# A fused decoder layer on one core: two sets of transposes go from TensorE to VectorE and small DMAs, and a state load is requested later

## The chip, the core and the metric

The kernel runs on one core of a Trainium2 chip. The metric is the device time of one execution in microseconds (us), as the median of three runs. The text calls the engines TensorE (PE, with its weight loads as PEld), VectorE (DVE), ScalarE (ACT), GpSimd (POOL) and SyncE (SP, which issues nearly all DMAs).

## What is computed

One layer of a decoder, in float32, for 256 prompt tokens with 16 meta tokens ahead of them and for 8 new tokens that each continue a stored state. The model width is 2048.

```
x <- LN1(alpha*x + 0.5*SwiGLU_1(x))
x <- LN2(alpha*x + Mixer(x))
x <- LN3(alpha*x + 0.5*SwiGLU_2(x))

Mixer: x @ w_in -> q_ret k_ret v_ret g_ret | q_hg f_hg i_hg g_hg | gate_ret gate_hg
  retention (8 heads of 256): S <- gamma*S + k^T v, o = (q k^T * decay) v + q S
  HGRN2 (16 heads of 128):    f = lb + (1-lb)*sigmoid(f_hg), k = 1 - f, q = silu(q_hg), v = i_hg
                              S <- f*S + k^T v, o = q S
  y = sigmoid(gate_ret)*LN(o_ret)*silu(g_ret) + sigmoid(gate_hg)*RMS(o_hg)*silu(g_hg);  y @ w_out
```

The outputs are the layer's result and both kinds of states, for the prompt and for the 8 new tokens.

## The kernel before, in words

**Dense products.** Activations lie with features on the partitions and the 280 tokens (16 + 256 + 8; 264 where the meta tokens are not needed) along the free axis. Every weight block of 128 x 128 and every activation tile is split into a high and a low part (`whi`, `wlo`; `xh`, `xl`), and `dense` issues three matmuls for a block: high x high, high x low, low x high (L218). Weights stream in loads of 8 blocks, 512 KB each, through three buffers: SP issues the DMA into `raw` (L185), ACT writes `whi` (L188), DVE writes `wlo` = `raw` - `whi` (L189), and PE then has 24 matmuls of such a load. A new `raw` can be issued when `wlo` of the load three before it is written.

**The mixing, by units.** `project` runs eight units u = 0 to 7, one retention head and two HGRN2 heads each. A unit is six groups of two 128-wide columns in the order f, q_h, i_h, q_r, k_r, v_r, and behind them come the four gate groups of the unit before: g_r/a_r, g_h/a_h, g_r/a_r, g_h/a_h. A group is 16 k-steps of six matmuls, four weight loads; a unit with its gates is 40 loads. `evacuate` takes a finished group out of PSUM.

**What sets the order.** The heads' own work is written as two generators, `mix_hg` (HGRN2) and `mix_ret` (retention), which `start` puts on a list with a delay. After each k-step `dense` calls `pump`, which counts every generator down by one and lets it issue its next piece at zero; a `yield n` is a pause of n k-steps. PE keeps exactly the order in which its instructions are written. The other engines' orders, SP's too, are set by a scheduler from priorities and from when it expects the operands; each engine then runs in order, and an instruction that waits holds up all behind it. A DMA completes on one of eight semaphores in turn, and an issue waits until the DMA that used its semaphore before has landed.

**HGRN2, unit u, before.** The evacuation of i_h copies the two heads' values to `v` (L667, L668) and starts `mix_hg` four k-steps later. It needs the values and the scaled keys `K` with tokens on the partitions. PE transposes the values, two blocks of 128 x 128 for each head (L875), into PSUM, and ACT copies them to `vt` (L879). The first and last 16 tokens of the values (`ends`, gathered by POOL) are transposed as one more block (L878). For K, `turned` does the same on PE (L982) and ACT (L983) into `kts`. These transposes are single matmuls against an identity. Then the state products `pst` = K^T v run on PE (L1022, L1024), ACT and DVE make the states `Sh` of them (L1025, L1027), and SP stores them (`out_sgp`). `samples` updates the 8 stored states of each head; `load` and `values` request what it needs, each held back by a one-column POOL copy into the buffer to be filled, which reads a tile that marks the time.

**Retention, unit u, before.** `mix_ret` starts three k-steps after v_r was evacuated. It requests the first half of the unit's stored states, two loads of 512 KB (`smr`, L1095), without a mark, so the scheduler puts them in SP's order as soon as the four `smr` buffers come free, behind the stores of the unit before (`out_srs`, L1202). Then come its transposes (L1107, L1114), scores (`psc`), state products (`psr`, L1168), and the update of the stored states: ACT scales them (L1192), DVE adds to them (L1198).

Of the kernel before, what the change touches and what calls it, by code (L numbers as in the profile page):

```python
# [18 lines left out]
P = 128  # L19
# [4 lines left out]
NMETA, SEQ, NS = 16, 256, 8  # L24
LP = NMETA + SEQ
T = LP + NS
# [102 lines left out]
def trunk(ctx: ExitStack, tc: tile.TileContext, A, O):  # L129
# [417 lines left out]
    with tc.tile_pool(name="yp", bufs=1) as yp:  # L547
# [7 lines left out]
        with tc.tile_pool(name="mp", bufs=1) as mp:  # L555
# [92 lines left out]
            def evacuate(n, c0, c1, o0, o1, b0, b1):  # L648
# [14 lines left out]
                elif n == "i_h":  # L663
                    v = st.pop("i_h", None)
                    if v is None:
                        v = tmp("v", (P, 2, T))
                        nc.scalar.copy(v[:, 0, :], o0)  # L667
                        nc.scalar.copy(v[:, 1, :], o1)  # L668

                    start(mix_hg(c0 // 2, st["f"], st["k"], st["q"], v), {0: 20, 2: 46}.get(c0, 4))  # L670
                elif n in ("q_r", "k_r"):
# [10 lines left out]
                elif n == "v_r":  # L682
                    v = tmp("v", (P, 2, T))
                    nc.scalar.copy(v[:, 0, :], o0)
                    nc.scalar.copy(v[:, 1, :], o1)
                    start(mix_ret(c0 // 2, st["q_r"], st["k_r"], v), 24 if c0 == 2 else 3)
                elif n in ("g_r", "g_h"):
# [14 lines left out]
                    else:  # L702
# [6 lines left out]
                        if c0 < EARLY:  # L709
                            split(yh[c0], yl[c0], y)  # L710

            NB2 = LP - 2 * P
            BLOCKS = ((0, P), (P, P), (2 * P, T - 2 * P))
# [31 lines left out]

            def mix_hg(u, f, k, q, v):

                calm = 2
                ends = tmp("ends", (P, 2, 2, NMETA))
                nc.gpsimd.tensor_copy(ends[:, :, 0, :], v[:, :, :NMETA])  # L750
                nc.gpsimd.tensor_copy(ends[:, :, 1, :], v[:, :, T - NMETA :])
                Q = tmp("Q", (P, 2, SEQ))
# [12 lines left out]
                def load(h):  # L765

                    sms.append(tmp("smh", (P, NS, P), bufs=2))
                    vbs.append(tmp("vbh", (P, NS, P), bufs=2))
                    nc.gpsimd.tensor_copy(sms[h][:, 0, :1], kts[0][:, 0, :1] if h else acc[:, 15:16])
                    nc.sync.dma_start(sms[h], A["sg"][2 * u + h])  # L770

                def values(h):
                    nc.gpsimd.tensor_copy(vbs[h][:, 0, :1], kts[1][:, 0, :1] if h else acc[:, 2 * P + 15 : 2 * P + 16])
                    nc.sync.dma_start(vbs[h], vrow[h].partition_broadcast(P))
# [93 lines left out]
                Q1 = side_by_side(1)  # L868
                vt = tmp("vth", (P, 2, 2, P))
                vrow = []  # L870
                for h in range(2):

                    pt = mx_bank("pt")
                    for b in range(2):
                        nc.tensor.transpose(pt[:, b * P : (b + 1) * P], v[:, h, NMETA + b * P : NMETA + (b + 1) * P], ident)  # L875
                    x = pt[:64, 2 * P : 3 * P]
                    if h:
                        nc.tensor.transpose(x, ends.rearrange("p c a t -> p (c a t)"), ident)  # L878
                    nc.scalar.copy(vt[:, h], pt[:, : 2 * P].rearrange("p (b f) -> p b f", b=2))  # L879
# [93 lines left out]
                on_h[u] = on  # L973
                kts = []

                def turned(h):
                    kt = tmp("kth", (P, 2, P), bufs=2)
                    kts.append(kt)
                    pt = mx_bank("ptk")
                    for b in range(2):  # L980
                        t0 = NMETA + b * P
                        nc.tensor.transpose(pt[:, b * P : (b + 1) * P], K[:, h, t0 : t0 + P], ident)  # L982
                    nc.scalar.copy(kt, pt[:, : 2 * P].rearrange("p (b f) -> p b f", b=2))  # L983
# [29 lines left out]
                if u != 1:  # L1013
                    samples(1)
                    yield 4 if u == 0 else 5

# [68 lines left out]
            def mix_ret(u, q, k, v):  # L1085
# [103 lines left out]
                for e in range(2):  # L1189
# [187 lines left out]
```

## Time and profile before

| what | value |
|---|---|
| runs, device time | 2566.4, 2569.12, 2565.67 us; median 2566.4 |
| profiled execution, first to last instruction | 2563.9 us |
| between that span and the median of the runs | 2.5 us |
| mean granted TensorE clock | 1.000 |
| PE, DVE, ACT, POOL busy, share of the span | 100%, 66%, 54%, 2% |
| DMA queue of SP | 532.37 MB, 62.0% of 16 engines' span |

The profile is of one execution. A row of the groups reads: line, engine, operation, out<-in, shape, count | busy us, mean ns of one | idle time of the engine before them, and what ended it. A row of the waits reads: engine and line <- what it waited for: us in total, times, longest. A row in order of time reads: start, length, engine, line, operation, out<-in, shape, count, all in us from the span's start. Matmul records overlap, since PE starts the next before the last has left the array: their lengths do not add up to time, their starts do. Line numbers are those of the kernel before.

### The profile page before, as it was taken

What the parts mean: (1) busy time and instruction counts of PE and PEld (TensorE: products, weight loads), DVE (VectorE), ACT (ScalarE), POOL (GpSimd) and SP (SyncE); (2) the same over time, 40 slices, a digit from 0 to 9 for tenths busy, and PEclk for the clock granted to TensorE, in tenths of its full rate; (3) what the DMA queues carried; (4) which work ended last, traced back from release to release, by engine and by line L of the source; (5) the groups of instructions that cost most, each with busy time, mean ns of one, the idle gap of its engine ahead of it and who ended that gap; (6) DMA issues with size and microseconds to landing.
All of it is one profiled execution on the core that took longest, in us unless ns stands there. A gap on an engine that the chain in (4) does not pass through costs nothing.

```text
span 2563.9 us, 56275 instructions
## 1 busy us (share of the span) xinstructions
PE 2553.4 (100%) x23424; PEld 2534.4 (99%) x23424; DVE 1702.8 (66%) x2827; ACT 1392.2 (54%) x2186; POOL 57.0 (2%) x152
## 2 busy tenths in 40 slices
PE   9999999999999999999999999999999999999999
PEld 9999999999999999999999999999999999999998
DVE  6444544475569878777777777777885555556555
ACT  5444444444456767767676666675564444444443
POOL 0000000000000000000000000000000000000000
PEclk9999999999999999999999999999999999999999
DMA  7555555555555876767676767675556565565554
GB/s 244 183 187 183 187 182 184 186 182 186 184 201 180 287 265 232 264 214 260 212 264 215 259 223 255 224 239 188 196 190 197 194 197 195 194 196 195 195 195 149
DMA packets 156897, 536.26 MB, mean 209 GB/s; under 512 B 17952, under 2 KB 25952, under 8 KB 156640
## 3 DMA queue, kind: packets, MB, share of 16 engines
q1 hardware_dynamic: 156352, 532.37, 62.0%
q8 instruction: 183, 3.00, 0.5%
q14 instruction: 74, 0.61, 0.1%
q10 hardware_dynamic: 288, 0.29, 0.0%
HBM read 501.99 MB, written 30.61 MB: 208 GB/s over the span
## 4 chain that ended last, share of the span: by engine, by line
PE 96%; DVE 2%; ACT 0%; issue 0%; DMA 0%; SPq 0%; ACTq 0%; DVEq 0%
PE up L218 36%; PE dn L218 19%; PE pj_i_h L218 3%; PE pj_g_r L218 3%; PE pj_q_h L218 3%; PE pj_g_h L218 3%; PE pj_a_r L218 3%; PE pj_a_h L218 3%; PE pj_f L218 3%; PE pj_q_r L218 3%; PE pj_k_r L218 3%; PE wo L218 3%; PE pj_v_r L218 3%; DVE wlo L189 1%; PE pqr L1211 1%; PE psr L1168 0%
## 5 line engine op out<-in xcount | busy, mean ns | idle before, releaser
L189 DVE TENSOR_TENSOR wlo<-raw,whi 128x1024 fp32r<-128x1024 f32 (+1 forms) x869 | 1062.2, 1223 | 740.7 <-ACT whi L188 737.3
L188 ACT CAST whi<-raw 128x1024 fp32r<-128x1024 f32 (+1 forms) x870 | 905.7, 1042 | 909.2 <-PE up L218 411.0
L218 PE MATMUL up<-xh,whi 128*128 128x280 f32 (+1 forms) x2624 | 725.6, 280 | 0.6 <-ACT whi L188 0.6
L218 PE MATMUL up<-xh,wlo 128*128 128x280 f32 (+1 forms) x2624 | 725.8, 280 | 0.4 <-DVE wlo L189 0.3
L218 PE MATMUL up<-xl,whi 128*128 128x280 f32 (+1 forms) x2624 | 725.4, 279 | 0.0
L218 PEld LDWEIGHTS up<-xh,wlo 128*128 128x128 f32 x2624 | 492.6, 189 | 1.0 <-DVE wlo L189 1.0
L218 PEld LDWEIGHTS up<-xh,whi 128*128 128x128 f32 x2624 | 492.6, 189 | 0.8 <-ACT whi L188 0.8
L218 PEld LDWEIGHTS up<-xl,whi 128*128 128x128 f32 x2624 | 492.6, 189 | 0.0
L218 PE MATMUL dn<-hh,whi 128*128 128x280 f32 (+1 forms) x1376 | 384.7, 280 | 0.0
L218 PE MATMUL dn<-hh,wlo 128*128 128x280 f32 (+1 forms) x1376 | 384.3, 279 | 0.0
L218 PE MATMUL dn<-hl,whi 128*128 128x280 f32 (+1 forms) x1376 | 384.3, 279 | 0.0
L218 PEld LDWEIGHTS dn<-hh,whi 128*128 128x128 f32 x1376 | 260.1, 189 | 0.1
L218 PEld LDWEIGHTS dn<-hl,whi 128*128 128x128 f32 x1376 | 260.1, 189 | 0.1
L218 PEld LDWEIGHTS dn<-hh,wlo 128*128 128x128 f32 x1376 | 260.1, 189 | 0.0
L218 PE MATMUL pj_k_r<-xh,whi 128*128 128x280 f32 x256 | 74.2, 290 | 0.0
L218 PE MATMUL pj_g_r<-xh,whi 128*128 128x264 f32 x256 | 74.0, 289 | 0.0
L218 PE MATMUL pj_v_r<-xh,whi 128*128 128x280 f32 x256 | 73.8, 288 | 0.0
L218 PE MATMUL pj_v_r<-xh,wlo 128*128 128x280 f32 x256 | 72.4, 283 | 0.3 <-DVE wlo L189 0.3
L218 PE MATMUL pj_g_h<-xh,whi 128*128 128x264 f32 x256 | 72.7, 284 | 0.0
L218 PE MATMUL pj_k_r<-xh,wlo 128*128 128x280 f32 x256 | 72.4, 283 | 0.0
L218 PE MATMUL pj_v_r<-xl,whi 128*128 128x280 f32 x256 | 72.3, 283 | 0.0
L218 PE MATMUL pj_k_r<-xl,whi 128*128 128x280 f32 x256 | 72.3, 283 | 0.0
(421 smaller groups left out, 5263.4 us busy)
## 6 DMA issues: line engine op xcount, KB each, us to landing
raw<-in_w_up SPq DMA_DIRECT2D x343, 512.0 KB, 4.1
raw<-in_w_in SPq DMA_DIRECT2D x320, 512.0 KB, 4.3
raw<-in_w_dn SPq DMA_DIRECT2D x172, 512.0 KB, 3.5
smr<-in_sr SPq DMA_DIRECT2D x32, 512.0 KB, 5.0
out_srs<-smr SPq DMA_DIRECT2D x32, 512.0 KB, 6.7
raw<-in_w_out SPq DMA_DIRECT2D x32, 512.0 KB, 3.9
vbr<-vrd SPq DMA_DIRECT2D x32, 256.0 KB, 4.1
smh<-in_sg SPq DMA_DIRECT2D x16, 512.0 KB, 5.2
```

The costliest lines, as they stand in the source:

```text
L188: nc.scalar.copy(hi[:, j:jn, :], raw[:, j:jn, :])
L189: nc.vector.tensor_tensor(out=lo[:, j0:j1, :], in0=raw[:, j0:j1, :], in1=hi[:, j0:j1, :].bitcast(F32), op=ALU.subtract)
L218: nc.tensor.matmul(o, w, t, start=start, stop=stop)
L1211: nc.tensor.matmul(pq[32 * j : 32 * j + 32, :256], qdr_at[c][:, 32 * b : 32 * b + 32], sms[2 * e + c][:, j, :], start=e + c == 0, stop=e + ...
```

## The change

From unit 2 on (the third unit):

- The evacuation of i_h no longer copies `v`. DVE transposes the two heads' 256 prompt tokens out of PSUM, in blocks of 32 x 32, into the tile `v`, and ACT copies the first and last 16 tokens of each head to `ends` (four copies of 16 columns).
- A 32 x 32 block is then turned but not at its place in the 128 x 128 block. `turned_over` puts it there by 16 DMAs on SP, each of 32 partitions x 4 runs of 32 elements (16 KB in runs of 128 bytes), one every two k-steps.
- K is turned in the same way by one DVE transpose of 512 columns at the place of the first PE transpose, into the tile that held `k`; 16 DMAs bring it into the tile that held `f`, which is `kts` now.
- PE's transposes of values and K go, with ACT's copies behind them. The one of `ends` stays.
- The pauses: `pst` comes 30 k-steps behind `samples(1)` instead of 5, and 20 instead of 45 follow it.
- Retention starts 5 k-steps after v_r instead of 3, and its pause before the sample scores is 13 instead of 15. Its first two state loads are marked by a POOL copy that reads `q`, so they go out only when the q_h group of their unit, which is the unit that follows the stores, has been evacuated.
- The POOL marks of HGRN2's second head read the turned `k` and a piece of `f`.

```diff
 elif n == "i_h":
-    v = st.pop("i_h", None)
-    if v is None:
+    v, vt = st.pop("i_h", None), tmp("vth", TURNED)
+    ends = tmp("ends", (P, 2, 2, NMETA))
+    if c0 > 2:
+        z = squared(tmp("v", (P, 2, T)))
+        for j, o in enumerate((o0, o1)):
+            nc.vector.transpose(z[:, j].rearrange("p b t -> p (b t)"), o[:, NMETA:LP])
+            nc.scalar.copy(ends[:, j, 0, :], o[:, :NMETA])
+            nc.scalar.copy(ends[:, j, 1, :], o[:, T - NMETA : T])
+        turned_over(vt, z, 2)
+    elif v is None:
...
-    start(mix_ret(c0 // 2, st["q_r"], st["k_r"], v), 24 if c0 == 2 else 3)
+    start(mix_ret(c0 // 2, st["q_r"], st["k_r"], v), {0: 3, 2: 24}.get(c0, 5))
...
+def turned_over(out, z, pause):
+
+    def transfers():
+        for i in range(0, P, 32):
+            for j in range(0, P, 32):
+                nc.sync.dma_start(out[j : j + 32, :, :, i : i + 32], z[i : i + 32, :, :, j : j + 32])
+                yield pause
+
+    start(transfers(), 1)
...
-    nc.gpsimd.tensor_copy(sms[h][:, 0, :1], kts[0][:, 0, :1] if h else acc[:, 15:16])
+    nc.gpsimd.tensor_copy(sms[h][:, 0, :1], (kts[0] if u < 2 else k)[:, 0, :1] if h else acc[:, 15:16])
...
-    kts = []
+    kts = [squared(f)[:, h] for h in range(2)] if u > 1 else []

     def turned(h):
+        if u > 1:
+            if h == 0:
+                z = squared(k)
+                nc.vector.transpose(z.rearrange("p h b t -> p h (b t)"), K[:, :, NMETA:])
+                turned_over(squared(f), z, 2)
+            return
...
     if u != 1:
         samples(1)
-        yield 4 if u == 0 else 5
+        yield 4 if u == 0 else 30
...
-    yield (8, 11, 45)[min(u, 2)]
+    yield (8, 11, 20)[min(u, 2)]
...
 def load(e):
     for c in range(2):
         sms.append(tmp("smr", (P, 4, 256), bufs=4))
+        if e == 0 and u > 1:
+            nc.gpsimd.tensor_copy(sms[c][:, 0, :1], st["q"][:, 0, :1])
         nc.sync.dma_start(sms[2 * e + c], A["sr"][u, c, :, 4 * e : 4 * e + 4, :])
...
-    yield (11 if u == 0 else 15) + 2 * calm
+    yield (11, 15, 13)[min(u, 2)] + 2 * calm
```

PE before, unit 4, at k-step 9 of the k_r group (`pj_k_r` are the group's two columns, `ptk` the transpose of K):

```order
L218 MATMUL pj_k_r_16261<-xh_9_9271,wlo_16376 128x280
L218 MATMUL pj_k_r_16262<-xh_9_9271,whi_16375 128x280
L218 MATMUL pj_k_r_16262<-xl_9_9272,whi_16375 128x280
L218 MATMUL pj_k_r_16262<-xh_9_9271,wlo_16376 128x280
L982 MATMUL ptk<-ident,K 128x128 x2
L218 MATMUL pj_k_r_16261<-xh_10_9275,whi_16375 128x280
```

After, the same place without it, in unit 4:

```order
L218 MATMUL pj_k_r_16304<-xh_9_9271,wlo_16423 128x280
L218 MATMUL pj_k_r_16305<-xh_9_9271,whi_16422 128x280
L218 MATMUL pj_k_r_16305<-xl_9_9272,whi_16422 128x280
L218 MATMUL pj_k_r_16305<-xh_9_9271,wlo_16423 128x280
L218 MATMUL pj_k_r_16304<-xh_10_9275,whi_16422 128x280
```

The pair is gone and nothing is in its stead; the same holds at step 13 and, for the values, at steps 3 and 4 of the q_r group.

PE before, unit 4, at k-step 13 of the v_r group, and after, behind k-step 6 of the first g_h/a_h gate group (`pst` are the state products; they read `f` for the turned keys now):

```order
L218 MATMUL pj_v_r_16461<-xh_13_9287,wlo_16598 128x280
L1022 MATMUL pst<-vm,km 128x128
L1024 MATMUL pst<-vth,kth 128x128 x2
L1022 MATMUL pst<-vm,km 128x128
L1024 MATMUL pst<-vth,kth 128x128 x2
L218 MATMUL pj_v_r_16460<-xh_14_9291,whi_16597 128x280
```

```order
L218 MATMUL pj_a_h_16896<-xh_6_9259,wlo_16974 128x264
L1050 MATMUL pst<-vm,km 128x128
L1052 MATMUL pst<-vth,f 128x128 x2
L1050 MATMUL pst<-vm,km 128x128
L1052 MATMUL pst<-vth,f 128x128 x2
L218 MATMUL pj_g_h_16895<-xh_7_9263,whi_16973 128x264
```

The ten matmuls of this row group (a float32 product is two matmuls, a float32r one is one) stand 25 k-steps later.

SP before and after, unit 4, over the same weight loads, which are the 31st to the 34th counted from the unit's first (`f<-k` are pieces of K, `vrd`, `vbr`, `out_srp` and `smr` retention's):

```order
L185 DMA raw_16972<-in_w_in 128x1024
L1156 DMA vbr<-vrd 128x512 x2
L185 DMA raw_17002<-in_w_in 128x1024
L1171 DMA out_srp<-sro 128x256
L185 DMA raw_17044<-in_w_in 128x1024
L1095 DMA smr<-in_sr 128x1024
L1171 DMA out_srp<-sro 128x256
L1095 DMA smr<-in_sr 128x1024
L185 DMA raw_17074<-in_w_in 128x1024
```

```order
L185 DMA raw_17020<-in_w_in 128x1024
L741 DMA f<-k 32x4x32 x5
L185 DMA raw_17062<-in_w_in 128x1024
L741 DMA f<-k 32x4x32
L749 DMA vrd<-vt_8636 8x256
L185 DMA raw_17104<-in_w_in 128x1024
L1186 DMA vbr<-vrd 128x512 x2
L1201 DMA out_srp<-sro 128x256
L1125 DMA smr<-in_sr 128x1024
L185 DMA raw_17134<-in_w_in 128x1024
```

The last six K pieces are ahead of the second and third of these weight loads, and retention's transfers are one to two loads later than before.

More of the change, by code (lines that the diff above doesn't have):

```diff
@@ L668, in evacuate @@
                         nc.scalar.copy(v[:, 1, :], o1)
-                    start(mix_hg(c0 // 2, st["f"], st["k"], st["q"], v), {0: 20, 2: 46}.get(c0, 4))
+                    start(mix_hg(c0 // 2, st["f"], st["k"], st["q"], v, ends, vt), {0: 20, 2: 46}.get(c0, 4))
                 elif n in ("q_r", "k_r"):
@@ L744, in sample_columns, with mix_hg @@
                     po[:, 3 * P :].rearrange("p (j c) -> p c j", c=32)[:, : 2 * n, :].rearrange("p (h e) j -> p h e j", e=2))
[L746 removed]
+            def mix_hg(u, f, k, q, v, ends, vt):
                 calm = 2
[L749 to L751 removed]
+                if u < 2:
+                    nc.gpsimd.tensor_copy(ends[:, :, 0, :], v[:, :, :NMETA])
+                    nc.gpsimd.tensor_copy(ends[:, :, 1, :], v[:, :, T - NMETA :])
                 Q = tmp("Q", (P, 2, SEQ))
@@ L768, in load @@
                     vbs.append(tmp("vbh", (P, NS, P), bufs=2))
-                    nc.gpsimd.tensor_copy(sms[h][:, 0, :1], kts[0][:, 0, :1] if h else acc[:, 15:16])
+                    nc.gpsimd.tensor_copy(sms[h][:, 0, :1], (kts[0] if u < 2 else k)[:, 0, :1] if h else acc[:, 15:16])
                     nc.sync.dma_start(sms[h], A["sg"][2 * u + h])
                 def values(h):
-                    nc.gpsimd.tensor_copy(vbs[h][:, 0, :1], kts[1][:, 0, :1] if h else acc[:, 2 * P + 15 : 2 * P + 16])
+                    n = 32 if h and u > 1 else P
+                    nc.gpsimd.tensor_copy(vbs[h][:n, 0, :1], kts[1][:n, 0, :1] if h else acc[:, 2 * P + 15 : 2 * P + 16])
                     nc.sync.dma_start(vbs[h], vrow[h].partition_broadcast(P))
@@ L868, in mix_hg @@
                 Q1 = side_by_side(1)
-                vt = tmp("vth", (P, 2, 2, P))
                 vrow = []
                 for h in range(2):
[L873 to L876, printed above, removed]
+                    if u < 2 or h:
+                        pt = mx_bank("pt")
+                    if u < 2:
+                        for b in range(2):
+                            nc.tensor.transpose(pt[:, b * P : (b + 1) * P], v[:, h, NMETA + b * P : NMETA + (b + 1) * P], ident)
                     if h:
+                        x = pt[:64, 2 * P : 3 * P]
                         nc.tensor.transpose(x, ends.rearrange("p c a t -> p (c a t)"), ident)
-                    nc.scalar.copy(vt[:, h], pt[:, : 2 * P].rearrange("p (b f) -> p b f", b=2))
+                    if u < 2:
+                        nc.scalar.copy(vt[:, h], pt[:, : 2 * P].rearrange("p (b f) -> p b f", b=2))
                     if h:
```

2 lines of the change are left out of this document (added).

## The prediction

> **What bounds the kernel now.** I read the page's busy times and chain first, then what TensorE (PE) waited for, then one unit's stretch, then single instructions.
>
> ```profile
> span 2563.9 us, 56275 instructions
> PE 2553.4 (100%) x23424; PEld 2534.4 (99%) x23424; DVE 1702.8 (66%) x2827; ACT 1392.2 (54%) x2186; POOL 57.0 (2%) x152
> ...
> PE 96%; DVE 2%; ACT 0%; issue 0%; DMA 0%; SPq 0%; ACTq 0%; DVEq 0%
> ```
>
> PE is busy for the whole span and is 96% of the chain that ended last. A busy PE need not be at its peak, so the next view is the list of what PE waited for, over the whole span:
>
> ```profile
> PE pw L515 <- DVE eps_h L163: 1.0, 1, 1.0
> PE pt L1116 <- POOL tails L1103: 0.9, 1, 0.9
> ...
> PE pj_v_r L218 <- DVE wlo L189: 0.3, 1, 0.3
> ```
>
> These are the two longest and a typical one of nine rows, together under 5 us in 2563.9. Asked for 980 to 1738 us alone, units 2 to 7, the same list is empty: there PE waits for nothing. One of those units (unit 4 in its mixing, 126 us) in the table by stage:
>
> ```profile
> 1232.00:1358.00 126.00, 126.00 (x1273) 124.33 (x1272) 98.18 (x193) 84.37 (x157) 6.18 (x14) 1.00 0.71 239
> ```
>
> The columns after the length are PE, PEld, DVE, ACT, POOL, the granted clock, the DMA share and GB/s. PE 126.00 of 126.00, clock 1.00, DVE 98.18. So an instruction taken out of PE's order there shortens the span by the time it holds the order up, as long as nothing else becomes late.
>
> **The change, part by part.** *Transposes leave PE.* In units 2 to 7 go four transposes of values (L875) and four of K (L982) each: 48, in 24 pairs. The groups by line, all eight units:
>
> ```profile
> L875 PE MATMUL pt<-ident,v 128*128 128x128 f32 x32 | 6.1, 273 | 0.0
> L982 PE MATMUL ptk<-ident,K 128*128 128x128 f32 x32 | 6.1, 273 | 0.0
> ```
>
> 273 ns is one record's length, but records overlap: what counts is how much later the next matmul starts. PE in order of time around one pair:
>
> ```profile
> 1266.08 0.28 PE L218 MATMUL pj_k_r<-xh,wlo 128*128 128x280 f32 x1
> ...
> 1266.43 0.28 PE L218 MATMUL pj_k_r<-xh,wlo 128*128 128x280 f32 x1
> 1266.56 0.38 PE L982 MATMUL ptk<-ident,K 128*128 128x128 f32 x2
> 1266.69 0.37 PE L218 MATMUL pj_k_r<-xh,whi 128*128 128x280 f32 x1
> 1266.89 0.28 PE L218 MATMUL pj_k_r<-xl,whi 128*128 128x280 f32 x1
> ...
> 1267.49 0.28 PE L218 MATMUL pj_k_r<-xh,whi 128*128 128x280 f32 x1
> ...
> 1268.68 0.28 PE L218 MATMUL pj_k_r<-xl,whi 128*128 128x280 f32 x1
> ```
>
> From 1266.08 to 1267.49, ten projection matmuls and the pair: 1.41. From 1267.49 to 1268.68, ten without: 1.19. The pair costs 0.22 us; both differences are rounded to 0.01, so 0.21 to 0.24. I take 0.225: 24 x 0.225 = **5.4 us**, bounds 24 x 0.21 = 5.0 and 24 x 0.24 = 5.8. The transpose of `ends` (64 rows) stays and is in neither.
>
> The Trainium skill says otherwise of the price: "TensorE: Matmul & The Clock Gate", Part 4 (PE-mode transpose), gives about 275 ns for a transpose in a kernel's context, which agrees with the 273 ns of a record here; summed by it the 48 would be worth an estimated 13.2 us. The spacing of the starts, not the record, decides between the two.
>
> *Copies and transposes on ACT and VectorE (DVE).* The rows for what goes and for the nearest of what comes:
>
> ```profile
> L668 ACT COPY v<-pj_i_h 128x280 f32<-128x280 f32 x7 | 2.8, 393 | 0.0
> L879 ACT COPY vth<-pt 128x256 f32<-128x256 f32 x16 | 5.6, 367 | 0.0
> L983 ACT COPY kth<-ptk 128x256 f32<-128x256 f32 x16 | 6.0, 373 | 8.2 <-PE ptk L982 8.1
> L1120 ACT COPY vt<-pt 24x128 f32<-24x128 f32 x16 | 4.1, 259 | 0.3
> L1083 DVE TENSOR_TENSOR vtr<-vtr,cen 128x512 f32<-128x512 f32 x8 | 5.5, 692 | 0.3
> L1083 DVE TENSOR_TENSOR osr<-osr,cen 128x256 f32<-128x256 f32 x8 | 3.4, 425 | 0.3
> ```
>
> Per unit ACT loses 2 x 0.393 (the row is one evacuation of two), 2 x 0.367 and 2 x 0.373, 2.3 us, and gains four small `ends` copies, at most 4 x 0.259 = 1.0: 1.3 us less. DVE gains two transposes of 256 columns and one of 512: no row shows one, and the nearest of the same sizes give 2 x 0.425 + 0.692 = 1.5 us; twice that would be 3.1. Either end fits in DVE's 126.00 - 98.18 = 28 us of room, and they stand ahead of the unit's tightest stretch (below), not in it. I price both at 0 on the path; without that room it would be up to 1.5 to 3.1 us a unit.
>
> *Thirty-two DMAs of 16 KB a unit on SP.* They finish what a 32 x 32 transpose leaves undone. Two questions: are weights (`raw`) late behind them, and are the turned pieces there when PE wants them. An issue, and what lands when:
>
> ```profile
> 1293.85 0.33 SPq L185 DMA_DIRECT2D raw<-in_w_in  x1
> ...
> 1302.99 0.33 SPq L185 DMA_DIRECT2D raw<-in_w_in  x1
> ```
> ```profile
> raw<-in_w_in SPq DMA_DIRECT2D x320, 512.0 KB, 4.3
> ...
> out_sgp<-Sh SPq DMA_DIRECT2D x16, 64.0 KB, 4.8
> ```
>
> At 0.33 us an issue, 32 are 10.6 us of SP's 126 a unit, at most six (2.0 us) between two weight loads, which come about one per 2.7 us or slower. In the order each issue also waits until the DMA eight issues before it has landed, 4.3 us for a `raw`. Against that stands the lead: the load that is read from 1312.2 on (below, counted at 24 projection matmuls to a load) was issued at 1302.99, 9 us ahead, and that is among the latest of the unit. Cost 0, up to 0.5 us a unit if not.
>
> For the second question: in SP's new order the last K piece stands behind the `raw` that before was issued at 1293.85, so it is out by about 1294.2 and, landing like the 64 KB store of 512-byte runs, there by 1299.0. PE wants it behind step 6 of the first g_h/a_h group, which ends where step 7 begins:
>
> ```profile
> 1303.39 0.28 PE L218 MATMUL pj_g_h<-xh,whi 128*128 128x264 f32 x1
> ```
>
> 4.4 us to spare: cost 0. The values' pieces are all issued ahead of the K pieces, whose start is the old place of L982 (1266.56); the buffer they are read from is next written after the v_r group, still running at 1282.64 (below). Cost 0. Behind PE's wait for a late piece stands its whole order; behind SP's, all weight loads.
>
> *The state matmuls and retention move.* The ten `pst` matmuls go from v_r step 13 into the gates, with two ACT copies and four DVE updates behind them; retention starts two steps later and gives them back at its last pause. Moved, they cost PE the same. What they push is the weight split in the gates, which is the tightest place of the unit:
>
> ```profile
> 1298.66 0.28 PE L218 MATMUL pj_g_h<-xh,whi 128*128 128x264 f32 x1
> ...
> 1312.39 0.28 PE L218 MATMUL pj_g_r<-xh,wlo 128*128 128x264 f32 x1
> ```
> ```profile
> 1310.97 1.22 DVE L189 TENSOR_TENSOR wlo<-raw,whi 128x1024 fp32r<-128x1024 f32 x1
> ```
> ```profile
> 1281.29 0.28 PE L218 MATMUL pj_v_r<-xh,wlo 128*128 128x280 f32 x1
> ...
> 1282.64 0.28 PE L218 MATMUL pj_v_r<-xl,whi 128*128 128x280 f32 x1
> ```
> ```profile
> L1027 DVE SCALAR_TENSOR_TENSOR Sh<-Sh,T,pst 128x128 f32<-128x128 f32 x32 | 9.1, 342 | 0.2
> L1025 ACT COPY Sh<-pst 128x128 f32<-128x128 f32 x16 | 3.5, 266 | 0.2
> ```
>
> Five loads of 24 matmuls (2.70 us each) after 1298.66, the sixth load's `wlo` is finished at 1312.19 and first read at 1312.39: 0.2 us to spare. Into this stretch go 4 x 0.342 = 1.4 us of DVE and 0.5 of ACT; PE gets there later by the ten `pst`, 1282.64 - 1281.29 less two matmuls of 0.12 = 1.1. So DVE loses 1.4 - 1.1 = 0.3 against 0.2 to spare. For it speaks that retention's own order changes: the weight casts now stand ahead of the two state scalings that ACT used to do first. I take 0; the other end is 1 us a unit.
>
> *First state loads behind the queries.* Two loads of 512 KB a unit move from right behind the last state stores to the q_h/i_h groups; nothing is added. POOL marks them, SP then issues; behind POOL's wait stand the marks for the HGRN2 states, much later. Loads cost PE nothing where they were, though ACT did wait for weights:
>
> ```profile
> ACT whi L188 <- DMA raw<-in_w_in: 40.7, 27, 3.1
> ```
>
> 40.7 us of such waits and none passed on to PE in units 2 to 7: 0, either sign, up to 0.5 us a unit (with the 32 DMAs above).
>
> **Sum.** 2563.9 - 5.4 = 2558.5 for the span. The median of the runs, 2566.4, is 2.5 above the profiled span, and nothing outside the span changes: 2566.4 - 5.4 = **2561.0 us**. 0.2% of this kernel, about what a measurement can tell from no change, is 5.1 us; the forecast is just past it.
>
> **The rivals.** *The gates' weight split becomes late* (0.2 us to spare, 0.3 lost): PE waits 0.5 to 1 us a unit, 3 to 6 in all: 2564 to 2567. Against it: the new order on ACT. 0.17.
>
> *Weights late behind small DMAs or the moved loads*, 0.5 us a unit: 3.0 back, 2564.0. For it: a DMA share of 0.71 already; against it, the long lead. 0.08.
>
> *PE makes no use of the time*, because DVE or DMA sets the pace in the gates anyway: 2566.4. Against it: PE's list of waits is empty there. 0.05.
>
> *The K pieces land too late* (slower). PE then stands at `pst`, its order behind it. With 4.4 us to spare on top of 4.8 us of landing, it begins at a landing of 9.2 us; it is slower than before by 0.2% from (5.4 + 5.1) / 6 = 1.75 us a unit, a landing of 11 us. At 12 us it costs 6 x 2.8 = 16.8: 2566.4 - 5.4 + 16.8 = 2577.8. For it: the runs are 128 bytes, and no row of before shows a turned transfer; against it: only 256 KB a unit. 0.06. The Trainium skill speaks for it: "VectorE: DVE Perf Modes", The three transpose paths, calls a plain DMA with a transposing pattern 19 times slower than the crossbar's 1309 ns where the destination's innermost stride is large, an estimated 25 us per 128 x 128; no run here shows it, and the runs of this change stay 32 elements long.
>
> *A transpose is worth its record*, 48 x 0.273 = 13.1: 2553.3. Against it: the spacing above. 0.03.
>
> **How the numbers follow.** My forecast 0.61. Its bounds 5.0 to 5.8 lie across the 5.1, mostly beyond: I give it 0.50 faster and 0.11 the same. Faster: 0.50 + 0.03 = 0.53. The same: 0.11 + 0.17 + 0.08 + 0.05 = 0.41. Slower: 0.06. The range takes in the forecast's bounds, the runs' own spread below (about 2 us), and above it the two rivals of late weights, up to 2565.8; outside stay the late pieces, the record's price and the upper end of the others, under 0.2. So 2558.8 to 2565.8.
>
> **What would show it.** Right: PE's order in units 2 to 7 shorter by 0.9 us each, its list of waits still empty from 980 us on, `wlo` still ahead in the gates. Wrong: PE waiting for DMA at `pst` (late pieces), for `wlo` or `whi` in the gates (late split), ACT waiting for `raw` for longer than 40.7 us and PE behind it, or a DVE transpose several times its 0.43 or 0.69 us.

## The result, and the profile after

| kernel | runs, us | median | profiled execution, span |
|---|---|---|---|
| before | 2566.4, 2569.12, 2565.67, 2569.96 | 2567.8 | 2563.9 |
| after | 2583.75, 2576.24, 2584.75, 2581.55 | 2582.65 | 2581.9 |

The change makes the kernel slower: the ratio after to before is 1.0055, 95% interval 1.0041 to 1.0070, 14.9 us by the medians. The forecast was 5.4 us faster. So beside the gain there is a loss of about 14.9 + 5.4 = 20.3 us, on average 3.4 us in each of the six changed units.

The head of the page, the busy times and the chain that ended last, after:

```profile
span 2581.9 us, 56449 instructions
PE 2556.8 (99%) x23376; PEld 2531.8 (98%) x23376; DVE 1709.3 (66%) x2845; ACT 1382.2 (54%) x2174; POOL 48.8 (2%) x152
...
PE 87%; DVE 6%; DMA 3%; ACT 2%; issue 1%; SPq 0%; POOL 0%; ACTq 0%; DVEq 0%; POOLq 0%
```

PE has lost its 48 transposes (23424 to 23376), and its part of the chain has fallen from 96% to 87%; DVE, DMA and ACT have taken it. What PE waits for, after:

```profile
PE pj_g_r L218 <- DVE wlo L189: 8.9, 9, 2.4
PE pj_g_h L218 <- DVE wlo L189: 2.6, 5, 0.9
PE pt L1146 <- POOL tails L1133: 1.9, 3, 0.9
```

The first two rows did not exist before: PE stands in the gates until DVE has split the weights. Where in a unit this happens is seen from the starts of the first matmul of every eighth weight load, from load 8 of unit 5 to its end. Before:

```profile
1360.62 0.28 PE L218 MATMUL pj_i_h<-xh,whi 128*128 128x280 f32 x1
...
1384.70 0.28 PE L218 MATMUL pj_k_r<-xh,whi 128*128 128x280 f32 x1
...
1410.29 0.28 PE L218 MATMUL pj_g_r<-xh,whi 128*128 128x264 f32 x1
...
1435.80 0.28 PE L218 MATMUL pj_g_r<-xh,whi 128*128 128x264 f32 x1
...
1464.48 0.28 PE L218 MATMUL pj_f<-xh,whi 128*128 128x280 f32 x1
```

After:

```profile
1371.21 0.28 PE L218 MATMUL pj_i_h<-xh,whi 128*128 128x280 f32 x1
...
1394.86 0.28 PE L218 MATMUL pj_k_r<-xh,whi 128*128 128x280 f32 x1
...
1418.89 0.28 PE L218 MATMUL pj_g_r<-xh,whi 128*128 128x264 f32 x1
...
1446.13 0.28 PE L218 MATMUL pj_g_r<-xh,whi 128*128 128x264 f32 x1
...
1476.83 0.28 PE L218 MATMUL pj_f<-xh,whi 128*128 128x280 f32 x1
```

The four stretches took 24.08, 25.59, 25.51 and 28.68 us before and 23.65, 24.03, 27.24 and 30.70 after. The first is 0.43 shorter: two pairs of transposes of values, 0.22 a pair, as priced. The second is 1.56 shorter: two pairs of K and the `pst` matmuls that have left it (1.56 - 0.44 = 1.12; in `moves_only` below, where PE still turns K, it is 1.12 shorter). The third, where those now stand, is 1.73 longer, 0.6 more than they explain, and the last eight loads, to which the change gives PE nothing, are 2.02 longer. That is the loss in this unit, 2.6 us against a gain of 0.87. On the Trainium skill's price of a transpose, about 275 ns in "TensorE: Matmul & The Clock Gate", Part 4, the spacing decides: a pair holds PE up by 0.22 us here, 0.11 each.

Behind the longest of those waits, in unit 6, DVE in order of time, after:

```profile
1567.31 0.48 DVE L1228 SCALAR_TENSOR_TENSOR smr<-vbr,k_r,smr 128x256 f32<-128x256 f32 x1 [2.38 <-DMA vbr<-vrd]
...
1578.08 0.88 DVE L1228 SCALAR_TENSOR_TENSOR smr<-vbr,sro,smr 128x256 f32<-128x256 f32 x2 [3.33 <-DMA vbr<-vrd]
1578.88 1.22 DVE L189 TENSOR_TENSOR wlo<-raw,whi 128x1024 fp32r<-128x1024 f32 x1
```

and ACT, after:

```profile
1570.20 1.15 ACT L1222 ACTIVATE smr<-smr,sro 128x1024 f32<-128x1024 f32 x1 [3.70 <-DMA smr<-in_sr]
...
1580.60 1.05 ACT L188 CAST whi<-raw 128x1024 fp32r<-128x1024 f32 x1 [3.83 <-DMA raw<-in_w_in]
```

Retention's updates of the stored states wait for their loads (`smr` on ACT) and for the rows of values that DMA spreads over the partitions (`vbr` on DVE); both engines run in order, and the weight cast or split stands behind the update. The chain at that place, in order of time, has the second pair of these `vbr` transfers, which stands behind a weight issue on SP:

```profile
1570.65 1.15 DVE wlo L189
...
1571.81 0.33 SPq L185
...
1572.19 5.80 DMA vbr<-vrd
...
1578.88 1.22 DVE wlo L189
```

Why the first pair is late is in SP's order of time, after, same place:

```profile
1553.85 4.21 SPq L741 DMA_DIRECT2D f<-k  x5
1558.16 0.53 SPq L185 DMA_DIRECT2D raw<-in_w_in  x1
1558.74 0.59 SPq L741 DMA_DIRECT2D f<-k  x1
1559.37 0.49 SPq L749 DMA_DIRECT2D vrd<-vt  x1
1562.20 0.33 SPq L185 DMA_DIRECT2D raw<-in_w_in  x1
1562.63 0.85 SPq L1186 DMA_DIRECT2D vbr<-vrd  x2
```

The last six pieces of K stand ahead of `vrd` and hold SP for 4.8 us: about 0.60 us for each issue, and 1.2 us of waits for earlier DMAs to land. The second pair needs the two buffers of the first, so it can go out only when DVE has read those. But this lateness is not the loss by itself: `vrd` is issued 5.95 us behind its data here (1553.42 to 1559.37), and 5.9 us behind it in `keys_gate_k` below, which is not measurably slower than the kernel before.

### The profile page after: what moved, and what is told of

Read it like the earlier page. It is cut to its first block, busy times and chain, and to the rows that moved or that the text cites. A ratio compares the mean times of both kernels' runs of the same rounds, so it can differ in the third digit from the quotient of the medians.

```text
span 2581.9 us, 56449 instructions
## 1 busy us (share of the span) xinstructions
PE 2556.8 (99%) x23376; PEld 2531.8 (98%) x23376; DVE 1709.3 (66%) x2845; ACT 1382.2 (54%) x2174; POOL 48.8 (2%) x152
## 4 chain that ended last, share of the span: by engine, by line
PE 87%; DVE 6%; DMA 3%; ACT 2%; issue 1%; SPq 0%; POOL 0%; ACTq 0%; DVEq 0%; POOLq 0%
PE up L218 36%; PE dn L218 19%; PE pj_q_h L218 3%; PE pj_f L218 3%; PE wo L218 3%; PE pj_i_h L218 3%; PE pj_q_r L218 3%; PE pj_k_r L218 2%; PE pj_g_h L218 2%; PE pj_a_h L218 2%; PE pj_g_r L218 2%; DVE wlo L189 2%; PE pj_a_r L218 2%; PE pj_v_r L218 2%; DMA vbr<-vrd 2%; DMA raw<-in_w_in 1%
## 5 line engine op out<-in xcount | busy, mean ns | idle before, releaser
L218 PE MATMUL pj_g_r<-xh,wlo 128*128 128x264 f32 x256 | 72.8, 285 | 9.9 <-DVE wlo L189 8.9
L218 PE MATMUL pj_g_h<-xh,wlo 128*128 128x264 f32 x256 | 71.3, 278 | 2.6 <-DVE wlo L189 2.6
```

The source lines that it names most:

```text
L218: nc.tensor.matmul(o, w, t, start=start, stop=stop)
```

## The experiments

The three parts of the change are called the turning (values and K by VectorE, with their pieces), the late sums (`pst` 25 k-steps later, 6.3 weight loads) and retention's delay (two k-steps) with its gate (the mark on the first state loads). My theory when I began (A) was the pieces on SP; the rivals were the late sums (B, F), the gate (E), the delay (G), both of these (C), and the small transfers themselves (D). All times are medians; before is 2567.0 to 2567.8 in the comparisons.

**The change taken apart.** `values_only` and `keys_only` turn one half on PE again, `moves_only` both. Late sums stay in `keys_only` and `moves_only`, gate and delay in `moves_only` alone. `values_only`, from the changed kernel, its core:

```diff
-                kts = [squared(f)[:, h] for h in range(2)] if u > 1 else []
+                kts = []
...
-                    yield 4 if u == 0 else 30
+                    yield 4 if u == 0 else 5
```

> The values' half alone: VectorE turns the values from the third unit on, TensorE still turns K, and the state sums, retention's delay and its state loads are where they were before. Its 24 transposes are worth 2.7 us by the prediction's 0.225 us a pair. Theory A (the 16 pieces of K stand ahead of retention's loads in SP's queue, retention's updates on VectorE wait for them, and the gates' weight split waits behind those): no piece of K, so 2564 to 2567.5 us, at or below before's 2567.8. Rival B (the state sums' VectorE work, moved into the gates, takes the weight split's slack): the same 2564 to 2567.5. Rival D (either half's small transfers cost as much, 20.3 us of loss in all, half of it here): 2567.8 - 2.7 + 10 = 2575.

> K's half alone: VectorE turns K, TensorE turns the values, the state sums stand late as in the changed kernel, but retention starts and loads as before the change. Theory A: nearly the whole loss, 2567.8 - 2.7 + 15 to 20 = 2580 to 2585 us. Rival B: the same. Rival C (the state loads that wait for the evacuated queries, and retention's two steps of delay, make the loss): 2565 us, the gain of 2.7 alone. Rival D: 2575.

> What the change moves, without any turning by VectorE: the state sums late in the gates, retention two steps later, its first state loads behind the queries; TensorE turns everything, no small transfers. Theory A: within 1 us of before, 2567 to 2569 us. Rival B or C: the loss without the gain, 2567.8 + 15 to 20 = 2583 to 2588 us.

Measured: `values_only` 2565.9 (ratio 0.9994, 0.9985 to 1.0003), `keys_only` 2569.0 (1.0006, 0.9997 to 1.0014), `moves_only` 2575.2 (1.0033, 1.0021 to 1.0044). Neither half carries the loss, against A and D; what is moved costs 7.8 us with no turning at all. But 7.8 and the two halves' costs (gain not reached: 2.7 - 1.5 = 1.2 and 2.7 + 1.6 = 4.3) are 13.3, though the late sums are counted twice in it, and not 20.3: the parts make each other worse. The moves carry 7.8 of the 20.3 us by themselves; the other 12.5 come only with the turning beside them.

**The pieces alone.** `dummy_keys` adds to the kernel before 16 transfers a unit of the shape and at the place of K's pieces, into a tile that nobody reads; `dummy_gate` lets the second load of HGRN2's rows of values wait for the first of them, as it does in the changed kernel.

```diff
+                                nc.sync.dma_start(sq(f)[j : j + 32, :, :, i : i + 32], sq(k)[i : i + 32, :, :, j : j + 32])
+                                yield 2
```

> The kernel before with 16 transfers a unit added from the third unit on, of the shape and at the place of K's pieces, from k into f, which nobody reads; TensorE turns everything, nothing moves. Theory A (SP's time is what costs): 10 to 20 us above before, 2578 to 2588 us. Rivals B and C: within 1 us of before, 2567 to 2569 us. Rival D: 2578.

> The kernel before with 16 idle transfers of the shape of K's pieces a unit (0.3 us above before in the run without more) and the second load of HGRN2's rows of values waiting for the first of them to land; TensorE turns everything and nothing else moves. Theory H: 2570 to 2575 us. Theories A and G: 2567 to 2569 us.

Measured 2567.7 (1.0003, 0.9994 to 1.0012) and 2568.5 (1.0005, 0.9996 to 1.0014). 16 issues and 16 transfers a unit cost nothing that can be measured where the rest stands as before. Theory A, in the form "SP's time is what costs", falls for this case; 32 pieces a unit, or pieces beside the moves, were not run without the turning.

**Gate or delay.** From the changed kernel: `no_gate`, `no_delay`, `no_gate_no_delay`; from the kernel before, with both or the one put in: `gate_delay_only`, `delay_only`.

```diff
-                        if e == 0 and u > 1:
-                            nc.gpsimd.tensor_copy(sms[c][:, 0, :1], st["q"][:, 0, :1])
```
```diff
-{0: 3, 2: 24}.get(c0, 5)
+24 if c0 == 2 else 3
...
-                yield (11, 15, 13)[min(u, 2)] + 2 * calm
+                yield (11 if u == 0 else 15) + 2 * calm
```

> The changed kernel without the gate on retention's first state loads (GpSimd's tiny copy of the evacuated queries into their tiles); retention still starts two steps later. Theory E (the gate: the state loads are asked for late, with the K pieces ahead of them in SP's queue, and retention's updates and the weight split behind them wait): most of the loss beyond the state sums' goes, 2569 to 2573 us. Rival F (the state sums in the gates, 6.3 loads later than before, take VectorE's slack there): little change, 2576 to 2581. Rival G (retention's delay of two steps puts its updates on top of the state sums): little change, 2577 to 2583.

> The changed kernel with retention started as early as before the change (3 steps after its values instead of 5, and the two steps given back to its later pause); the gate stays. Theory E: little change, 2578 to 2584 us. Rival F: 2578 to 2583. Rival G: most of the loss goes, 2569 to 2573.

> The changed kernel without the gate and without the delay: both halves of the turning, the state sums late. If the parts add up as the runs so far show them (values cost 1.2 us against their 2.7, K with the late sums 4.3 against its 2.7), 2567.5 - 5.4 + 1.2 + 4.3 = 2567.6 us, so 2565 to 2570. Theories E and G both allow that. Rival F (the late sums alone make the loss): 2575 to 2581.

> The kernel before with the gate on retention's first state loads and the delay of two steps, and nothing else: TensorE turns everything, the state sums stand where they stood. Theory E or G: most of the 7.8 us that all three moves cost together, 2572 to 2576 us. Rival F: none of it, 2567 to 2569 us. If only the gate, the delay and the late sums together cost, each under 2 us alone: 2567 to 2570.

> The kernel before with retention's start two steps (half a weight load) later and the two steps given back in its later pause; no gate, no turning by VectorE, state sums where they were. Theory G (the gates' weight split has no time to spare, and what is moved towards it comes out at PE): 2574 to 2578 us, what the gate and the delay cost together (2576.7). Theory E (the gate): 2567 to 2569 us.

Measured: `no_gate` 2581.1 (1.0055, 1.0042 to 1.0067), `no_delay` 2575.9 (1.0032, 1.0021 to 1.0043), `no_gate_no_delay` 2577.2 (1.0036, 1.0024 to 1.0049), `gate_delay_only` 2576.7 (1.0036, 1.0023 to 1.0048), `delay_only` 2575.8 (1.0032, 1.0019 to 1.0044). The gate is worth nothing either way: 2582.65 to 2581.1, 2575.9 to 2577.2, 2576.7 to 2575.8, each pair with intervals that overlap. E falls. **The delay alone costs 8.6 us** in a kernel where PE turns everything, which is 1.4 us a unit, 0.8 to 1.9 by the interval. Taking it out of the changed kernel gives 6.7 back, and 3.8 where the gate is out too; in these two pairs the intervals still touch. `no_gate_no_delay` missed its sum (2567.6) by 9.6: both halves together with the late sums, without gate and delay, lose what neither half lost alone.

What the delay does, ACT in order of time in unit 5, before:

```profile
1429.08 1.15 ACT L1192 ACTIVATE smr<-smr,sro 128x1024 f32<-128x1024 f32 x1 [0.36 <-DMA smr<-in_sr]
1430.13 1.03 ACT L188 CAST whi<-raw 128x1024 fp32r<-128x1024 f32 x1
1431.13 1.15 ACT L1192 ACTIVATE smr<-smr,sro 128x1024 f32<-128x1024 f32 x1
```

and with the delay alone, where the unit runs 4.15 us later (the first matmul of its 27th weight load stands at 1416.68 before and at 1420.83 here):

```profile
1436.60 1.15 ACT L1213 ACTIVATE smr<-smr,sro 128x1024 f32<-128x1024 f32 x1 [2.35 <-DMA smr<-in_sr]
1437.65 1.03 ACT L188 CAST whi<-raw 128x1024 fp32r<-128x1024 f32 x1
1439.31 1.15 ACT L1213 ACTIVATE smr<-smr,sro 128x1024 f32<-128x1024 f32 x1 [0.63 <-DMA smr<-in_sr]
```

The second pair of state loads can be asked for only when `psr` has read the tiles that it goes into. Half a weight load later for `psr` becomes 3.4 us for ACT's first scaling of that pair (1436.60 - 1429.08 - 4.15). SP issues the first of these loads 1.65 us later (1424.40 before, 1430.20 here); the rest is its landing. PE's list of waits of that kernel has a new first row:

```profile
PE pj_g_r L218 <- DVE wlo L189: 4.6, 5, 1.3
```

The chain that ends in one of these waits, in unit 6, with the delay alone:

```profile
1557.45 6.32 DMA smr<-in_sr
...
1564.93 1.04 ACT whi L188
...
1566.00 1.24 DVE wlo L189
...
1567.25 0.33 SPq L185
...
1567.62 4.84 DMA vbr<-vrd
...
1572.89 1.23 DVE wlo L189
```

The state load holds ACT's scaling (1563.88), the cast stands behind that and the split behind the cast. The split frees a buffer for SP's next weight issue, and behind that issue in SP's order stands a `vbr` transfer, for which DVE's updates and the next split wait. In four of the five waits the chain ends with this `vbr`, and in three of them (units 4, 6 and 7) it comes from the state load; in unit 5 it comes from PE. In the kernel before, both `vbr` of this pair follow one weight issue (1429.70 in unit 5); with the delay a weight issue stands between them (1436.24 and 1440.34).

ACT's wait for these loads is not the loss by itself. In `keys_gate_k` below it is as long (19.5 us in all against 19.4, and 2.13 and 0.75 in unit 5), the two `vbr` go out together (1433.16), and that kernel is not measurably slower than before. That the delay's price comes through this order of SP is read from the traces; no run changed the order alone. By size the price is close to the delay's own length: two k-steps are half of 2.70 us, 1.35, against 1.4 measured.

**SP's stand.** In the changed kernel the second load of values on SP (L794) waits until POOL has marked its tile, and POOL waits for the first piece of K to land; behind it stand the weights and 14 pieces. The list of waits, after, which names the last of POOL's instructions each time:

```profile
SPq L794 <- POOL meta L1018: 13.2, 2, 7.0
SPq L794 <- POOL vbh L793: 10.2, 3, 4.6
...
SPq L794 <- POOL tails L1133: 8.2, 2, 4.6
```

`vb_gate_k` marks it from `k`, which VectorE has turned earlier; `vb_gate_k_plain` does so without gate and delay, `keys_gate_k` in K's half alone.

```diff
-nc.gpsimd.tensor_copy(vbs[h][:n, 0, :1], kts[1][:n, 0, :1] if h else ...)
+nc.gpsimd.tensor_copy(vbs[h][:, 0, :1], (kts[1] if u < 2 else k)[:, 0, :1] if h else ...)
```

> The changed kernel with one operand of one tiny copy changed: the second load of HGRN2's rows of values waits for k as VectorE has turned it, and no longer for the first piece of K to have landed, for which SP stood 31.6 us in all in the changed kernel. Theory H (SP's standing wait at that load, with 14 pieces and the weights behind it, bunches the pieces in front of retention's loads): 2567 to 2574 us, the rest being the delay's. Theory G (retention's two steps of delay are the loss) and theory A (the issue time of the pieces themselves): 2578 to 2584, little changed.

> The same edit, and also neither the gate on the state loads nor the delay: what is left of the change is the turning, its pieces and the late state sums. Theory H: before's 2567.5 less a good part of the 5.4 us of transposes, 2562 to 2567 us. Theory A: 2573 to 2579, as without the edit (2577.2).

> K's half alone, state sums late, no gate, no delay, and the second load of values waiting for k as VectorE has turned it instead of the first piece of K (for which SP stood 13.9 us in all in K's half alone). If that stand costs the K half: 2565 to 2567 us against its 2569.0. If not: 2568 to 2570.

Measured 2580.2 (1.0052, 1.0039 to 1.0065), 2573.3 (1.0023, 1.0014 to 1.0032) and 2567.3 (1.0000, 0.9991 to 1.0009): 2.5, 3.9 and 1.7 us less than the same kernels with the stand, which adds up to 31.6 us in the changed one. Each pair's intervals overlap. So the stand costs little of what it looks like, and H, as the cause of the loss, falls; `vb_gate_k_plain` lies in the range that A had for it (2573 to 2579).

**Another queue.** `pool_plain` and `act_plain` are `vb_gate_k_plain` with all pieces issued by GpSimd or by ScalarE.

```diff
-nc.sync.dma_start(out[j : j + 32, :, :, i : i + 32], z[i : i + 32, :, :, j : j + 32])
+nc.scalar.dma_start(out[j : j + 32, :, :, i : i + 32], z[i : i + 32, :, :, j : j + 32])
```

> The kernel of the run before with all 32 pieces a unit asked for from GpSimd's queue and none from SP's, so that SP carries what it carried before the change. Theory A (the pieces' 0.6 us of SP each): 2561 to 2565 us, and below the run with the pieces on SP by 3 us or more. Theory H: within 2 us of that run. If the small transfers load the DMA engines themselves: no better than it, 2570 or more in both.

> Both halves turned by VectorE, no gate, no delay, the second load of values not waiting for K's pieces, and all 32 pieces a unit asked for from ScalarE's queue instead of SP's. Theory A2 (pieces standing in SP's order, bunched behind weight loads that wait for their buffer, delay the next weights and state loads): 2562 to 2567 us against 2573.3 with the pieces on SP. Theory D (the transfers themselves slow the weights): 2572 to 2576. If an issue costs ScalarE as much as SP (0.6 us, 19 us a unit ahead of its weight casts): 2585 or more.

Measured 2588.1 (1.0086, 1.0072 to 1.0099) and 2599.9 (1.0125, 1.0111 to 1.0139), 14.8 and 26.6 us above the pieces on SP. What ACT's casts wait for in `act_plain`:

```profile
ACT whi L188 <- DMA f<-k: 53.2, 15, 5.1
...
ACT whi L188 <- DMA raw<-in_w_in: 31.9, 27, 3.3
```

The casts stand 53.2 us behind pieces: a queue on a busy engine puts the pieces into that engine's order. In `pool_plain` ACT and DVE wait 24.6 and 21.4 us for an operation on POOL (`meta`, L1017), waits that the list of `vb_gate_k_plain` does not have. So these runs don't tell issue from transfer. The Trainium skill says that DMAs issued by different engines run on the same 16 DMA engines and that issuing from several saves only the time to initiate them ("DMA: Bandwidth & Descriptors", Issuing engines are not separate DMA queues). Both runs agree that nothing is gained, and show what the sentence leaves out, what the new issuer loses.

**The late sums.** `values_late_sums` is `values_only` with 30 and 20 k-steps for the sums as in the change.

> The values' half alone with the state sums moved 6.3 loads later as in the changed kernel; TensorE turns K. If the late sums cost nothing: 2565 to 2567 us, as the values' half alone (2565.9). If they take VectorE's time in the gates (rival F, priced at 1 us a unit): 2571 to 2573.

Measured 2571.5 (1.0017, 1.0008 to 1.0026), 5.6 above `values_only`: rival F's price, with the loss mostly elsewhere than it had it: PE waits 4.4 us where retention begins and 1.2 in the gates. PE's list of waits in `values_late_sums`, first two rows:

```profile
PE pt L1138 <- POOL tails L1125: 2.8, 3, 1.0
PE pt L1129 <- ACT v L691: 1.6, 2, 0.9
```

In the kernel before, the ten `pst` matmuls stood 4 us ahead of that place (1408.4 to 1412.3 in unit 5).

**A later second half.** Two kernels, `later_second` from the changed one and `plain_later_second` from `vb_gate_k_plain`, were to give the second state loads four more k-steps to land.

```diff
-                    yield 1 if e else 10 if u == 0 else 6
+                    yield 1 if e else (10, 6, 10)[min(u, 2)]
```

> The changed kernel with one number of pacing changed: retention's second half (the scaling by ScalarE and the updates by VectorE of the second pair of states) is asked for 10 steps behind the first instead of 6, one weight load later, and the four steps are taken from the pause behind it. Theory J (ScalarE stands 29.6 us in all at that scaling until the second pair of state loads has landed, and the gates' weight casts stand behind it): that wait falls below 12 us, and the time to 2567 to 2573 us. If the weights' own lateness (69.4 us of casts that wait for the transfer, 40.7 before) carries the loss: 2577 to 2583 us, with the wait gone all the same. If the later updates collide with the matmuls that read the states: above 2585.

> Both halves turned by VectorE, no gate, no delay, the second load of values not waiting for K's pieces (2573.3 us so far), and the second half four steps later as in the run before. Theory J: 2564 to 2569 us, ScalarE's wait for the second pair down from 24.5 us to under 10. If the weights' own lateness carries what is left (74.8 us of casts that wait for the transfer): 2571 to 2575.

Measured 2581.7 (1.0061, 1.0047 to 1.0074) and 2572.8 (1.0021, 1.0012 to 1.0030), their parents' times within 1 us. But this decides nothing on theory J. In `later_second` ACT's wait for the states is still 28.7 us, and in both kernels the orders of ACT, DVE, POOL and SP are the parent's, row for row: the pause did not reach the scaling. They are repeats of their parents, no test. They do show how far a sum of waits varies between executions of one order: 16.9 us in `plain_later_second` against 24.5 in its parent.

**All in one table.** Waits in us over one profiled execution of each, from the lists of waits: PE in the gates for the weight split; PE at retention's transposes for `tails` and `v`; ACT for retention's states; DVE for `vbr`; ACT's casts for `raw` of `w_in`.

| kernel | median - before | PE, gates | PE, retention | ACT, `smr` | DVE, `vbr` | ACT, `raw` |
|---|---|---|---|---|---|---|
| before | 0 | 0 | 0.9 | 7.4 | 1.8 | 40.7 |
| `values_only` | -1.5 | 1.1 | 0.9 | 6.6 | 6.1 | 47.1 |
| `values_late_sums` | +4.4 | 1.2 | 4.4 | 9.3 | 6.0 | 48.1 |
| `keys_only` | +1.6 | 0.9 | 1.1 | 21.0 | 7.8 | 42.1 |
| `keys_gate_k` | +0.1 | 0.3 | 1.9 | 19.5 | 5.2 | 52.9 |
| `delay_only` | +8.6 | 4.8 | 0.9 | 19.4 | 6.8 | 36.3 |
| `no_gate_no_delay` | +9.8 | 1.6 | 6.4 | 21.1 | 8.8 | 64.2 |
| after | +14.9 | 11.5 | 1.9 | 29.6 | 27.5 | 69.4 |

PE's listed waits are less than the loss, as its starts show some tenths more around each of them, and as some profiled executions were faster than their median (2573.1 us for `delay_only`, 2572.7 for `no_gate_no_delay`); they tell where the loss is. There are two places. Both halves with the late sums make PE wait where retention starts (6.4). The two k-steps of delay take that wait away (1.9) and put a larger one into the gates (11.5): the changed kernel has bought the one with the other.

## Why the prediction was wrong

The steps in its order:

- *Transposes leave PE*, 0.225 us a pair: right. The starts give 0.22 for values and the same for K.
- *Copies and transposes on ACT and VectorE*, taken at 0.425 and 0.692 us from the nearest rows: right. DVE's two forms in the changed kernel, min, median and max in ns:

```profile
L669 DVE STREAM_TRANSPOSE v<-pj_i_h x12: 405/425/443, 996.3 to 1641.2; 128x256 f32<-128x256 f32 x12
...
L1002 DVE STREAM_TRANSPOSE k<-K x6: 702/704/705, 1016.2 to 1659.6; 128x512 f32<-128x512 f32 x6
```

- *Thirty-two DMAs of 16 KB a unit*, 0.33 us an issue: the issue was mis-sized, min, median and max of it in ns:

```profile
L741 SPq DMA_DIRECT2D vth<-v x96: 591/599/1847, 997.1 to 1655.7; - x96
L741 SPq DMA_DIRECT2D f<-k x96: 585/599/1653, 1019.0 to 1688.4; - x96
```

  That is 19.2 us of SP a unit, not 10.6, and six pieces with their waits took 4.8 us, not 2.0. Alone, 16 of them cost 0.3 us in all (-1.5 to 3.1 by the interval). Beside the moves this step's "cost 0, up to 0.5 us a unit" does not hold: 12.5 us, 2.1 a unit, come where turning and moves stand together, and the runs don't tell the issues, the transfers and the changed orders apart. The other question of that step, whether K's pieces are there at `pst`, was answered rightly: PE has no wait for them, and the rival of late pieces did not come.
- *The state matmuls and retention move*, "I take 0; the other end is 1 us a unit": **this is the step that failed.** It weighed the late sums (0.3 us lost against 0.2 to spare) and took retention's two k-steps as free, even as a help, because the weight casts would stand ahead of the state scalings. Measured, the two k-steps cost 1.4 us a unit by themselves (8.6 / 6), and the late sums 0.9 beside the values' half (5.6 / 6); with the gate the moves cost 7.8 in all. The step counted what enters the stretch and not what is asked for behind `psr`: the second state loads move with it, and by the trace a cast, a split, a weight issue on SP and a `vbr` transfer behind them, in a stretch that had 0.2 us to spare.
- *First state loads behind the queries*, 0 either sign: right, by three pairs of kernels.
- *The rivals.* "The gates' weight split becomes late" is what came, with a chance of 0.17 and a price of 0.5 to 1 us a unit. Its place and kind were right; the size was on average 3.4 us a unit, most of it in the gates, since it held only DVE's 0.3 against 0.2 and none of the waits for loads that retention's order carries. The one rival on the slower side was another mechanism, so the range did not reach there. Two of the signs named for being wrong did come: PE waits for `wlo` in the gates, and ACT's wait for `raw` is 69.4 us instead of 40.7.

What was also wrong is that the terms were added. Each was held against the spare time of the kernel before by itself: 32 issues, a later `pst`, a later retention. By the traces they draw on the same spare time of the weights, and `keys_only` plus `values_only` (+0.1) against both together with the late sums (+9.8) shows how far from a sum it is. Of these 9.7 us 5.9 come with the late sums beside the values' half (`values_late_sums`, +4.4 against -1.5, each beside the kernel before of its own comparison), and 3.8 are left for both halves together.

What stays open is the cause of these 9.7 us. The trace of `no_gate_no_delay` shows a bunch of pieces on SP ahead of a weight load and state loads,

```profile
1389.03 5.11 SPq L741 DMA_DIRECT2D vth<-v  x6
1394.24 1.66 SPq L185 DMA_DIRECT2D raw<-in_w_in  x1
```

then a cast that waits for its load, and the evacuation of v_r behind it on ACT, with PE waiting 0.84 us for `tails` at the end (1418.08):

```profile
1403.64 1.05 ACT L188 CAST whi<-raw 128x1024 fp32r<-128x1024 f32 x1 [2.95 <-DMA raw<-in_w_in]
```

That load was issued at 1396.94 and by the chain took 6.60 us to land, where the median of a weight load before is 4.3. In `keys_only` the cast at this place waits for no load. Whether the bunch on SP or the load on the DMA engines makes it late was not separated: the runs on other queues brought waits of their own. That `pst`, ahead of retention's transposes, used to cover ACT's lateness there fits `values_late_sums`, but is only argued. And the way of the delay's cost through the second state loads and `vbr` is read from the trace; the kernel that was to take ACT's wait away did not. No version here is measurably faster than before; the best, `values_only`, has an interval that holds 1.

## What to carry to other kernels

A pipeline with a few tenths of a microsecond to spare at its tightest place has one budget, not one for each edit: add up all that an edit delays, on every in-order queue, ahead of that place, and price the sum, not the terms. A shift of half a weight load is not free because the matmuls stay as many: here it cost about its own length. Follow what is requested behind it, when it lands, and what stands behind the engine that waits for it; and look for a kernel that has the same wait without the loss before calling the wait the cause. Look at the orders, too, after changing a pause: where a scheduler decides, the pause may move nothing.

## What was not expected of the hardware

- An issue of 32 partitions x 4 runs of 128 bytes takes SP 0.599 us, one of 128 x 4 KB 0.33 us. The number of bytes is 32 times smaller and the issue longer. Six issues in a row, with their waits, took 5.11 us in `no_gate_no_delay`, and the next weight issue 1.66, where the longest before took 0.66.
- The Trainium skill calls the generation of descriptors "small, variable" among the parts of a DMA's fixed cost ("DMA: Bandwidth & Descriptors", Anatomy of one DMA, which is of GpSimd's path). On SP here the issue is 0.599 us, on GpSimd's queue in `pool_plain` 0.551; how much of it is descriptors no run shows.
- VectorE's transpose of 128 x 512 in 32 x 32 blocks takes 0.704 us, and 0.425 us for 128 x 256 out of PSUM, about as long as a subtraction of the same size (0.692 and 0.425).
